# A layer with routed experts: the test for left-over blocks moves behind the output, and the output's tiles change their order

## The chip, the cores and the metric

One core of a Trainium2 chip runs the whole kernel. The metric is the time of one execution on the device, in microseconds; the median of several runs counts. TensorE (PE) multiplies matrices and transposes, VectorE (DVE), ScalarE (ACT) and GpSimd (POOL) compute on tiles of 128 partitions, SyncE (SP) issues most of the DMA transfers. Each of them works through its own list of instructions in order, and they wait for one another by semaphores.

## The reference

One layer over 1024 latent tokens of width 1024 and 256 context tokens: a token mixer (an mLSTM part and a convolution part), then a mixture of 64 experts of which every token takes 8, with one shared expert. Float32 throughout. What the change touches is the end:

```python
def body(acc, xs):
    rows, rw, e = xs
    xb = hpad[rows]
    y = (jax.nn.silu(xb @ we_gate[e]) * (xb @ we_up[e])) @ we_down[e]
    return acc.at[rows].add(y * rw[:, None].astype(y.dtype)), None
...
shared = (jax.nn.silu(hf @ ws_gate) * (hf @ ws_up)) @ ws_down
return (acc[:nt] + shared).reshape(B, T, D)
...
x = x + mx[5] * _rms_norm(_moe_ffn(hx, ...), g_post_ffn[l])
```

## The kernel before, in words

`Full.run` calls `front` and `mixer_out` (the mixer and the routing), then `moe`, `spill` and `final`. The change lies in the last three.

**The schedule.** How many rows each expert gets is known only on the chip. The program is built with fixed capacities: a table of blocks (`BLOCKS`) of up to 128 rows, each with its expert's rank by load. The routing gives the blocks their experts and rows. What does not fit into the table is left over; `route` counts the blocks of 128 rows that it makes up into `nl`.

**The blocks.** `pipeline` runs over the table: gather rows of `hx` from DRAM, transpose them (`stage_x`: transposes on TensorE into `px`, a rounded copy `xH` by ScalarE, the remainder `xL` by VectorE), multiply with gate and up weights (`stage_gu`: 24 matmuls of 512 columns into `pgu`, SiLU into `sgu`, product `hgu`), transpose the result (`stage_ht`: `pht`, then `hTH` and `hTL`), multiply with the down weights (`stage_dn`: 12 matmuls into `py`), and add the rows to one of two arrays in DRAM, `acc0` or `acc1`, by an accumulating scatter from POOL. A product of full precision is three matmuls of rounded parts (`mm3`, lines 436 to 438). The shared expert of token tiles 0 to 3 (`SE = 4`) is in the table, that of tile 3 as its last block, whose result is added to rows 384 to 511 of `acc1` by a plain accumulating DMA (line 1557). That of tiles 4 to 7 is left to the end. `pipeline` closes with loads for the end: the rows `h` of tiles 4 to 7 and `x1`, the residual, of all eight; and it transposes tiles 4 and 5.

**The left-over blocks.** `spill` reads `nl` from memory into a register on every engine and branches over its body where `nl` is 0. The body makes up the lists of rows again and loops over the blocks, one expert's weights each, adding to `acc0`. In this data nothing is left over, and the body is not run.

```python
nl = nc.values_load(self.nl[0:1, 0:1], min_val=0, max_val=128)
with tc.If(nl > 0):
```

**The output.** `final` goes over the eight tiles in their order. For each, `sums` loads its 128 rows of `acc0` and `acc1` (`v0`, `v1`; three buffers each, `VB = 3`). Tiles 4 to 7 get their shared expert: `gu` one tile ahead, then `stage_ht` and 12 matmuls, and VectorE adds the two halves `py` to `v0` (line 1727). Then VectorE adds `v1` (line 1729), and `rms_apply` makes the output: squares summed on ScalarE (line 1143), the product with the weight `vg` on POOL (line 1145; for the last tile on VectorE), the power -1/2 of the mean on POOL (line 1147, `ssf`), and `u`, the scaled product plus `x1`, on VectorE (line 1148). SP stores it (line 1732). The squares and `vg` have one buffer each:

```python
junk, t = [fp.tile([128, D], F32, name=m, bufs=1) for m in ("sq", "vg")]
```

**What orders the work.** Within a stretch of straight code a scheduler puts each engine's instructions into an order of its own, by what depends on what and its estimate of their times. It does not move them over a branch. Every engine follows that order, and waits where its next instruction has to.

Of the kernel before, what the change touches and what calls it, by code (L numbers as in the profile page):

```python
# [869 lines left out]
SE = 4  # L870
# [9 lines left out]
NA = 2  # L880
VB=3
# [4 lines left out]
class Full(Layer):  # L886
    known = SH

    def run(self):
        nc, tc, A = self.nc, self.tc, self.A  # L890
        cp, cp_ = self.pool("const", 1)
        dp, dp_ = self.pool("dram", 1, DRAM)
        self.hx = dp.tile([NX, XW], F32, name="hxd")
        self.x1d = dp.tile([NX, D], F32, name="x1d")
        self.posd = dp.tile([128, 8, NE], F32, name="posd")
        self.acc = [dp.tile([NX, D], F32, name=f"acc{k}") for k in range(NA)]
        self.rowd = dp.tile([2, NR, 128], F32, name="rowd")
        self.amd = dp.tile([4, D], F32, name="amd")
        ct, ct_ = self.pool("ctmp", 1)
        self.consts(cp, ct)  # L900
        self.route_consts(cp, ct)
        self.close(ct_)
        X = self.front(cp)
        self.mixer_out(cp, X)
        self.moe(cp)
        self.spill()
        self.final(cp)
        self.close(self.fin_)
        self.close(dp_)
        self.close(cp_)  # L910
# [49 lines left out]
    def mixer_out(self, cp, X):  # L960
# [45 lines left out]
        pI = pp.tile([128, HM * NE], F32, name="pI")  # L1006
        run = cp.tile([128, NE], F32, name="run")
        nc.vector.memset(run, 0.0)
        self.run = run
        r8 = lambda v: v.rearrange("p (k t) -> p k t", k=8)  # L1010
# [61 lines left out]
        def place(j, pl, mask, eq):  # L1072


            mm(pl[:, 1], self.sub, mask, start=True, stop=True)
            mm(pl[:, 2], self.onb, mask, start=True, stop=True)
            nc.vector.tensor_tensor(self.pos[:, j], pl[:, 1], run, op=OP.add)
            nc.vector.tensor_tensor(run, run, pl[:, 2], op=OP.add)
            m = tp.tile([128, TK, NE], F32, name="m")
            (nc.vector if j == 7 else nc.gpsimd).tensor_tensor(  # L1080
                m, eq, self.pos[:, j].unsqueeze(1).to_broadcast([128, TK, NE]), op=OP.mult)
            p8 = tp.tile([128, 3, TK], F32, name="p8")
            nc.vector.tensor_reduce(p8[:, 0], m, axis=AX.X, op=OP.add)
            pi = tp.tile([128, 2, TK], I32, name="pi")
            nc.vector.tensor_copy(pi[:, 0], p8[:, 0])
            nc.vector.tensor_scalar(pi[:, 1], pi[:, 0], -HB, None, op0=OP.bitwise_and)
            nc.vector.tensor_tensor(p8[:, 1], p8[:, 0], pi[:, 1], op=OP.subtract)
            nc.vector.tensor_tensor(p8[:, 2], self.f8[:, j], pi[:, 1], op=OP.add)
            oh = tp.tile([128, TK, HB], BF, name="oh")
            nc.vector.tensor_tensor(oh, self.io[:, :HB].unsqueeze(1).to_broadcast([128, TK, HB]), e8(p8[:, 1]),  # L1090
                                    op=OP.is_equal)
            l1 = tp.tile([128, TK, 128], BF, name="l1")
            nc.scalar.activation(l1[:, :, :HB], oh, AF.Identity, scale=self.pc)
            nc.gpsimd.tensor_scalar(l1[:, :, HB:], oh, float(j), None, op0=OP.mult)
            g = tp.tile([128, TK, HM * NE], BF, name="g", bufs=1)
            for k in range(TK):
                n = HM * NE if j + k == 0 else min(2 * (j + 1), HM) * NE
                nc.vector.tensor_scalar(g[:, k, :n], self.ioh[:, :n], p8[:, 2, k:k + 1], None, op0=OP.is_equal)
            return l1, g
# [147 lines left out]
    def spill(self):  # L1247

        nc, tc, A = self.nc, self.tc, self.A
        mm = nc.tensor.matmul  # L1250
        nl = nc.values_load(self.nl[0:1, 0:1], min_val=0, max_val=128)
        with tc.If(nl > 0):
# [47 lines left out]
            x = T("oxg", [128, XW])  # L1300
            nc.vector.memset(x, 0.0)
            with tc.For_i(0, nl, 1) as i:
# [20 lines left out]
                h = T("oh", [128, DE])  # L1323
# [16 lines left out]
                                             bounds_check=NX - 1, oob_is_err=False, compute_op=OP.add)  # L1340
            self.close(tp_)
            self.close(op_)

    def row_weight(self, junk, x, e, out):

        n = out.shape[0]
        self.nc.vector.scalar_tensor_tensor(junk[:n], self.io[:n, :NE], e[:n], x[:n, D:], op0=OP.is_equal, op1=OP.mult,  # L1347
                                            accum_out=out)
# [215 lines left out]
    def pipeline(self, experts):  # L1564

        nc, mp = self.nc, self.mp
        n, total = len(BLOCKS), 3 * len(experts)
# [64 lines left out]
        def row(key):  # L1632

            if not self.halves:
                t = take(F32, "rows", 0, NF)
                self.halves = [t[:, :D], t[:, D:]]
            self.rows[key] = self.halves.pop()
            return self.rows[key]
# [49 lines left out]
        split(total, True)  # L1688
        for j in range(SE, 8):
            nc.sync.dma_start(row(("h", j)), self.hx[128 * j:128 * j + 128, :D])  # L1690
        self.x = {j: self.stage_x(self.rows["h", j]) for j in range(SE, min(SE + 2, 8))}
        for j in range(8):
            nc.sync.dma_start(row(("x", j)), self.x1d[128 * j:128 * j + 128])
        self.shared = [W[3 * shared + c] for c in range(3)]


    def final(self, cp):
        nc, tc, A = self.nc, self.tc, self.A
        fp, fp_ = self.pool("last", 2)

        def sums(j):
            out = []
            for k in range(NA if j < 8 else 0):
                out.append(fp.tile([128, D], F32, name=f"v{k}", bufs=VB))
                nc.sync.dma_start(out[k], self.acc[k][128 * j:128 * j + 128])  # L1705
            return out

        def gu(j):
            if j + 2 < 8:
                self.x[j + 2] = self.stage_x(self.rows["h", j + 2])  # L1710
            return self.stage_gu(self.x[j], self.shared)

        V = [sums(n) for n in range(VB - 1)]
        if SE < 8:
            h = gu(SE)
        for j in range(8):
            V.append(sums(j + VB - 1))
            v, x1 = V[j], self.rows["x", j]
            if j >= SE:
                hT = self.stage_ht(h)  # L1720
                if j < 7:
                    h = gu(j + 1)
                for q in range(2):
                    py, s = self.bank("py", 512), slice(512 * q, 512 * q + 512)
                    for k in range(2):
                        self.mm6(py, hT, self.shared[2], k, 2, slice(k * 1024 + q * 512, k * 1024 + q * 512 + 512))
                    nc.vector.tensor_tensor(v[0][:, s], v[0][:, s], py, op=OP.add)  # L1727
            for u in v[1:]:
                nc.vector.tensor_tensor(v[0], v[0], u, op=OP.add)  # L1729
            junk, t = [fp.tile([128, D], F32, name=m, bufs=1) for m in ("sq", "vg")]  # L1730
            self.rms_apply(fp, v[0], self.fin, x1, junk, t, x1, "f", nc.gpsimd if j < 7 else None)
            nc.sync.dma_start(self.out[128 * j:128 * j + 128], x1)
        self.close(fp_)
        for _, p in self.pps[::-1]:
            self.close(p)
        for _, p in self.units[NF - 1:1:-1]:
            self.close(p)
        self.close(self.mp_)
        for _, p in self.units[1::-1]:
            self.close(p)  # L1740
        self.close(self.gp_)
# [69 lines left out]
```

## Time and profile before

| | |
|---|---|
| median of 3 runs | 1500.9 us (1499.1 to 1502.76) |
| profiled execution | 1497.91 us |
| its span, first to last instruction | 1496.1 us |
| mean granted TensorE clock | 0.986 |
| busy: PE, DVE, ACT, POOL | 1426.1, 1133.3, 753.7, 477.9 us |

The profile is of one execution. An engine's busy time says little about a short stretch: over the whole run TensorE is busy 95% of the span, but the change concerns some 65 us at its end, from the last expert block to the last store. There the order of time of each engine and the chain of waits tell more. Times in rows count from the span's start. "PEldq", "DVEq" and so on are the sequencers of the engines, which read registers, branch and wait for semaphores; "SPq" is the queue of SP, where DMA transfers are issued.

### The profile page before, as it was taken

To read this page: it belongs to the slowest core of one execution; us is meant where nothing else is said; L and a number is where in the kernel's file an instruction comes from. 1 tells how busy PE (TensorE), PEld (TensorE's weight loads), DVE (VectorE), ACT (ScalarE), POOL (GpSimd) and SP (SyncE) were. 2 spreads that over 40 slices of the span, in tenths; PEclk is the share of its full clock that TensorE was granted. 3 is DMA by queue.
4 is the path that set the end of the run, shared out by engine and by line. 5 is a ranking of instruction groups with operands and counts; after the bars stand their busy time and mean duration, and the time that the engine had idled before them with its cause. 6 is when DMAs were issued, how large, how long until landed. Compare 5 with 4: busy or idle time off the path is not lost. (4 is left out here: it accounts for less than half of the span.)

```text
span 1496.1 us, 22962 instructions
## 1 busy us (share of the span) xinstructions
PE 1426.1 (95%) x8211; PEld 1088.5 (73%) x8211; DVE 1133.3 (76%) x1942; ACT 753.7 (50%) x1241; POOL 477.9 (32%) x306
## 2 busy tenths in 40 slices
PE   6999999989999989999999999999999999999975
PEld 4688997765567755876788888888777777777764
DVE  5899979767867886744678788888777877777636
ACT  4421011245433344644566666776676767666621
POOL 1245001112213422233333333333334344455324
PEclk9999999999999999999999999999999999999998
DMA  8421051018653567997999999999999999999975
GB/s 314 176 71 43 1 189 40 19 48 287 221 187 115 193 240 275 357 294 246 306 288 327 331 322 319 333 343 339 316 342 299 321 342 310 315 352 318 337 251 209
DMA packets 94385, 371.64 MB, mean 248 GB/s; under 512 B 18269, under 2 KB 26789, under 8 KB 67770
## 3 DMA queue, kind: packets, MB, share of 16 engines
q1 hardware_dynamic: 65946, 298.48, 53.3%
q0 software_dynamic: 26032, 70.19, 19.2%
q10 hardware_dynamic: 2288, 1.45, 0.4%
q8 instruction: 66, 1.08, 0.3%
q14 instruction: 53, 0.43, 0.1%
HBM read 322.38 MB, written 62.19 MB: 257 GB/s over the span
## 5 line engine op out<-in xcount | busy, mean ns | idle before, releaser
L51 DVE TENSOR_TENSOR u<-u,u 128x1024 fp32r<-128x1024 f32 x354 | 422.0, 1220 | 124.7 <-ACT u L50 94.8
L50 ACT CAST u<-u 128x1024 fp32r<-128x1024 f32 x354 | 361.3, 1052 | 108.5 <-PE pgu L438 41.6
L1559 POOL DMA_INDIRECT acc<-yb,dst x98 | 194.4, 1983 | 351.7 <-ACT hTH L50 118.3
L436 PE MATMUL pgu<-u,xH 128*128 128x512 f32 x608 | 245.8, 404 | 0.4
L437 PE MATMUL pgu<-u,xH 128*128 128x512 f32 x608 | 238.8, 393 | 0.0
L438 PE MATMUL pgu<-u,xL 128*128 128x512 f32 x608 | 238.1, 392 | 0.0
L1439 POOL DMA_INDIRECT xg<-hxd,tok x98 | 123.6, 1261 | 194.1 <-DVE rwj L1347 68.6
L431 DVE SCALAR_TENSOR_TENSOR X<-X,cw 128x912 f32<-128x912 f32 (+14 forms) x120 | 152.0, 1291 | 1.1
L436 PEld LDWEIGHTS pgu<-u,xH 128*128 128x128 f32 x608 | 114.5, 188 | 25.5 <-ACT u L50 2.6
L438 PEld LDWEIGHTS pgu<-u,xL 128*128 128x128 f32 x608 | 114.3, 188 | 24.6
L437 PEld LDWEIGHTS pgu<-u,xH 128*128 128x128 f32 x608 | 114.5, 188 | 21.5
L436 PE MATMUL py<-u,hTH 128*128 128x512 f32 x304 | 122.1, 402 | 0.5 <-ACT hTH L50 0.5
L437 PE MATMUL py<-u,hTH 128*128 128x512 f32 x304 | 119.8, 394 | 0.0
L438 PE MATMUL py<-u,hTL 128*128 128x512 f32 x304 | 118.6, 395 | 0.0
L436 PE MATMUL pf<-hH,wfH 128*128 128x512 f32 x256 | 103.6, 408 | 0.0
L437 PE MATMUL pf<-hL,wfH 128*128 128x512 f32 x256 | 102.7, 401 | 0.7 <-DVE hL L226 0.6
L51 DVE TENSOR_TENSOR xL<-px,xH 128x512 fp32r<-128x512 f32 x152 | 97.5, 681 | 7.7 <-ACT xH L50 7.3
L438 PE MATMUL pf<-hH,wfL 128*128 128x512 f32 x256 | 102.3, 400 | 0.0
L50 ACT CAST xH<-px 128x512 fp32r<-128x512 f32 x152 | 83.9, 592 | 13.7 <-PE pgu L437 7.8
L1551 DVE COPY yb<-py 128x512 f32<-128x512 f32 x75 | 51.5, 687 | 46.3 <-PE py L438 45.8
L51 POOL TENSOR_TENSOR wfL<-wfr,wfH 128x1024 fp32r<-128x1024 f32 x14 | 48.0, 3428 | 118.2 <-ACT wfH L50 104.2
L1461 PE MATMUL px<-ident,xg 128*128 128x128 f32 x600 | 83.8, 274 | 1.1 <-DVE nl L1244 1.1
(431 smaller groups left out, 2515.6 us busy)
## 6 DMA issues: line engine op xcount, KB each, us to landing
u<-in_we_dram SPq DMA_DIRECT2D x192, 1024.0 KB
wa<-in_wa_dram SPq DMA_DIRECT2D x64, 256.0 KB
wa<-in_wa_dram SPq DMA_DIRECT2D x8, 1024.0 KB
wfr<-in_wf_dram SPq DMA_DIRECT2D x16, 512.0 KB
v<-acc SPq DMA_DIRECT2D x16, 512.0 KB
acc<-zero SPq DMA_DIRECT2D x13, 512.0 KB
u<-in_ws_dram SPq DMA_DIRECT2D x6, 1024.0 KB
X<-in_xT_dram SPq DMA_DIRECT2D x8, 512.0 KB
```

Of the source, the lines that this page charges most:

```text
L50: self.nc.scalar.copy(H, src)
L51: return (eng or self.nc.vector).tensor_tensor(L, src, H.bitcast(F32), op=OP.subtract).ins
L431: nc.vector.scalar_tensor_tensor(y[:, :, a:b], u[:, :, a + o:b + o], cw[:, i:i + 1], y[:, :, a:b], op0=OP.mult, op1=OP.add)
L436: mm(out, lH, rH, start=start, stop=False, skip_group_check=free)
L437: mm(out, lH, rL, start=False, stop=False, skip_group_check=free)
L438: mm(out, lL, rH, start=False, stop=stop, skip_group_check=free)
L1439: nc.gpsimd.indirect_dma_start(out=x[:n], out_offset=None, in_=self.hx, in_offset=bass.IndirectOffsetOnAxis(ap=self.tok[:n, c:c + 1], axis=0),
L1461: nc.tensor.transpose(pt[:, k], x[:, (4 * q + k) * 128:(4 * q + k) * 128 + 128], self.ident)
L1551: nc.vector.tensor_copy(y[:, 512:], py)
L1559: nc.gpsimd.indirect_dma_start(out=self.acc[b % NA].rearrange("r (n d) -> (r n) d", n=n), in_=y[:rows], in_offset=None, out_offset=bass.In ...
```

## The change

`spill` is called behind the output. The output's loop moves from `final` into a function of its own, `tiles`, which `final` calls first; the body of `spill` then loads `x1` again and calls `tiles` a second time, so that with blocks left over the whole output is made again. The first transposes of tiles 4 and 5 move from `pipeline` into `tiles`. And the tiles come in the order 4, 0, 5, 1, 6, 2, 7, 3: `order` puts one of the tiles that need the shared expert ahead of each that doesn't. POOL's product is now made for all but the last in that order, which is tile 3.

```diff
--- before.py
+++ after.py
@@ -903,7 +903,6 @@
         X = self.front(cp)
         self.mixer_out(cp, X)
         self.moe(cp)
-        self.spill()
         self.final(cp)
         self.close(self.fin_)
         self.close(dp_)
@@ -1340,6 +1339,9 @@
                                              bounds_check=NX - 1, oob_is_err=False, compute_op=OP.add)
             self.close(tp_)
             self.close(op_)
+            for j in range(8):
+                nc.sync.dma_start(self.rows["x", j], self.x1d[128 * j:128 * j + 128])
+            self.tiles()
 
     def row_weight(self, junk, x, e, out):
 
@@ -1688,34 +1690,38 @@
         split(total, True)
         for j in range(SE, 8):
             nc.sync.dma_start(row(("h", j)), self.hx[128 * j:128 * j + 128, :D])
-        self.x = {j: self.stage_x(self.rows["h", j]) for j in range(SE, min(SE + 2, 8))}
         for j in range(8):
             nc.sync.dma_start(row(("x", j)), self.x1d[128 * j:128 * j + 128])
         self.shared = [W[3 * shared + c] for c in range(3)]
 
 
-    def final(self, cp):
-        nc, tc, A = self.nc, self.tc, self.A
+    def tiles(self):
+
+
+        nc = self.nc
         fp, fp_ = self.pool("last", 2)
+        order = [j for k in range(8 - SE) for j in (SE + k, *range(k * SE // (8 - SE), (k + 1) * SE // (8 - SE)))]
+        later = [j for j in order if j >= SE]
+        x = {j: self.stage_x(self.rows["h", j]) for j in later[:2]}
 
         def sums(j):
             out = []
-            for k in range(NA if j < 8 else 0):
+            for k in range(NA):
                 out.append(fp.tile([128, D], F32, name=f"v{k}", bufs=VB))
                 nc.sync.dma_start(out[k], self.acc[k][128 * j:128 * j + 128])
             return out
 
         def gu(j):
             if j + 2 < 8:
-                self.x[j + 2] = self.stage_x(self.rows["h", j + 2])
-            return self.stage_gu(self.x[j], self.shared)
-
-        V = [sums(n) for n in range(VB - 1)]
-        if SE < 8:
-            h = gu(SE)
-        for j in range(8):
-            V.append(sums(j + VB - 1))
-            v, x1 = V[j], self.rows["x", j]
+                x[j + 2] = self.stage_x(self.rows["h", j + 2])
+            return self.stage_gu(x.pop(j), self.shared)
+
+        h = gu(SE)
+        V = [sums(j) for j in order[:VB - 1]]
+        for n, j in enumerate(order):
+            if n + VB - 1 < 8:
+                V.append(sums(order[n + VB - 1]))
+            v, x1 = V[n], self.rows["x", j]
             if j >= SE:
                 hT = self.stage_ht(h)
                 if j < 7:
@@ -1728,9 +1734,13 @@
             for u in v[1:]:
                 nc.vector.tensor_tensor(v[0], v[0], u, op=OP.add)
             junk, t = [fp.tile([128, D], F32, name=m, bufs=1) for m in ("sq", "vg")]
-            self.rms_apply(fp, v[0], self.fin, x1, junk, t, x1, "f", nc.gpsimd if j < 7 else None)
+            self.rms_apply(fp, v[0], self.fin, x1, junk, t, x1, "f", nc.gpsimd if n < 7 else None)
             nc.sync.dma_start(self.out[128 * j:128 * j + 128], x1)
         self.close(fp_)
+
+    def final(self, cp):
+        self.tiles()
+        self.spill()
         for _, p in self.pps[::-1]:
             self.close(p)
         for _, p in self.units[NF - 1:1:-1]:
```

What this makes of the engines' lists is seen at three places. Buffers carry numbers: before, `v0_15113`, `15117`, `15166`, `15208` and `15222` are tiles 0, 1, 2, 5 and 6; in the changed kernel `v0_14529`, `14533`, `14537` and `14619` are tiles 4, 0, 5 and 1.

SP, from the test on, before (ahead of it stand the loads of `x1`, and between them and this piece the body that is skipped):

```order
L1252 UNCONDITIONAL_BRANCH
L1705 DMA v0_15113<-acc0_63 128x1024
L1705 DMA v1_15115<-acc1_64 128x1024
L1705 DMA v0_15117<-acc0_63 128x1024
L1705 DMA v1_15119<-acc1_64 128x1024
L1705 DMA v0_15166<-acc0_63 128x1024
L1705 DMA v1_15168<-acc1_64 128x1024
L1732 DMA out_0_dram<-u6_14465 128x1024
```

The same place in the changed kernel, from the last loads of `x1` on:

```order
L1694 DMA u8_14439<-x1d_61 128x1024 x2
L1694 DMA u11_14442<-x1d_61 128x1024 x2
L1711 DMA v1_14531<-acc1_64 128x1024
L1711 DMA v1_14535<-acc1_64 128x1024
L1711 DMA v1_14539<-acc1_64 128x1024
L1711 DMA v0_14529<-acc0_63 128x1024
L1711 DMA v0_14533<-acc0_63 128x1024
L1711 DMA v0_14537<-acc0_63 128x1024
L1711 DMA v1_14621<-acc1_64 128x1024
L1711 DMA v1_14635<-acc1_64 128x1024
L1711 DMA v0_14619<-acc0_63 128x1024
```

The branch is gone from between the loads of `x1` and those of the sums, `acc1` comes first for three tiles, then `acc0`, and tile 4 is the first of each three.

VectorE, its first instructions behind the test, before (`px_15123` and `px_15130` are the transposed halves of tile 6, `pgu_15137` belongs to tile 4):

```order
L1729 TENSOR_TENSOR v0_15113<-v0_15113,v1_15115 128x1024
L1146 TENSOR_SCALAR ssf_15173<-ssf_15173 128x1
L1148 SCALAR_TENSOR_TENSOR u6_14465<-vg_15172,ssf_15173,u6_14465 128x1024
L51 TENSOR_TENSOR xL_15122<-px_15123,xH_15121 128x512
L51 TENSOR_TENSOR xL_15122<-px_15130,xH_15121 128x512
L1498 TENSOR_TENSOR hgu_15164<-pgu_15137,sgu_15162 128x256
L1729 TENSOR_TENSOR v0_15117<-v0_15117,v1_15119 128x1024
L1729 TENSOR_TENSOR v0_15166<-v0_15166,v1_15168 128x1024
```

In the changed kernel, behind the second half of tile 5's split (`px_14486` and `px_14493` are tile 6, `px_14550` and `px_14557` tile 7; `pgu_14500` and `pgu_14564` belong to tiles 4 and 5):

```order
L51 TENSOR_TENSOR xL_14469<-px_14477,xH_14468 128x512
L1735 TENSOR_TENSOR v0_14533<-v0_14533,v1_14535 128x1024
L51 TENSOR_TENSOR xL_14485<-px_14486,xH_14484 128x512
L51 TENSOR_TENSOR xL_14485<-px_14493,xH_14484 128x512
L1500 TENSOR_TENSOR hgu_14527<-pgu_14500,sgu_14525 128x256
L51 TENSOR_TENSOR hTL_14545<-pht_14541,hTH_14544 128x256
L51 TENSOR_TENSOR xL_14549<-px_14550,xH_14548 128x512
L51 TENSOR_TENSOR xL_14549<-px_14557,xH_14548 128x512
L1500 TENSOR_TENSOR hgu_14591<-pgu_14564,sgu_14589 128x256
L1733 TENSOR_TENSOR v0_14529<-v0_14529,py_14593 128x512
```

One sum, that of tile 0, still stands ahead of tile 6's split; the sums of the next two tiles and the first output have gone from behind it, and the work of tiles 4 and 5 takes their place.

VectorE in the middle of the output, before, from tile 5's output to tile 6's sum:

```order
L1148 SCALAR_TENSOR_TENSOR u8_14471<-vg_15362,ssf_15363,u8_14471 128x1024
L1498 TENSOR_TENSOR hgu_15404<-pgu_15377,sgu_15402 128x256
L1727 TENSOR_TENSOR v0_15222<-v0_15222,py_15406 128x512
L1727 TENSOR_TENSOR v0_15222<-v0_15222,py_15414 128x512
L51 TENSOR_TENSOR hTL_15436<-pht_15432,hTH_15435 128x256
L1729 TENSOR_TENSOR v0_15222<-v0_15222,v1_15224 128x1024
```

In the changed kernel, from tile 4's output to tile 5's sum (`py_14673` and `py_14681` are tile 5's halves, `pgu_14644` belongs to tile 6):

```order
L1147 SCALAR_TENSOR_TENSOR u8_14439<-vg_14611,ssf_14612,u8_14439 128x1024
L1145 TENSOR_SCALAR ssf_14626<-ssf_14626 128x1
L1147 SCALAR_TENSOR_TENSOR u6_14433<-vg_14625,ssf_14626,u6_14433 128x1024
L1500 TENSOR_TENSOR hgu_14671<-pgu_14644,sgu_14669 128x256
L1733 TENSOR_TENSOR v0_14537<-v0_14537,py_14673 128x512
L1735 TENSOR_TENSOR v0_14619<-v0_14619,v1_14621 128x1024
L1733 TENSOR_TENSOR v0_14537<-v0_14537,py_14681 128x512
L51 TENSOR_TENSOR hTL_14721<-pht_14717,hTH_14720 128x256
L1735 TENSOR_TENSOR v0_14537<-v0_14537,v1_14539 128x1024
```

Two outputs now follow each other, those of tiles 4 and 0, and behind the second stand the product of tile 6, both halves and the sum of tile 5, and the sum of tile 1.

## Rows read from the trace of the kernel before

**Rows 1.** TensorE in order of time: start, us, engine, line, operation, tiles, [idle before]

```profile
1431.30 0.82 PE L1461 MATMUL px<-ident,u 128*128 128x128 f32 x6
...
1439.93 1.94 PE L1461 MATMUL px<-ident,u 128*128 128x128 f32 x8 [6.20 <-DVEq L1252]
...
1465.60 0.39 PE L436 MATMUL pgu<-u,xH 128*128 128x512 f32 x1
1465.84 0.39 PE L437 MATMUL pgu<-u,xH 128*128 128x512 f32 x1
```

**Rows 2.** Sequencers at lines 1251 and 1252: ns min/median/max, first and last start

```profile
L1251 DVEq TENSOR_LOAD <-nl x1: 1719/1719/1719, 1434.4 to 1434.4; - x1
...
L1252 PEldq COMPARE_BRANCH  x1: 5473/5473/5473, 1433.7 to 1433.7; - x1
...
L1252 DVEq EVENT_SEMAPHORE  x1: 21/21/21, 1439.7 to 1439.7; - x1
```

**Rows 3.** Waits of the DMA queue of SP, 1405 to 1445: us, times, longest

```profile
SPq L1705 <- DVEq L1252: 4.7, 1, 4.7
```

**Rows 4.** Chain of waits, in order of time: start us, us, what

```profile
1442.70 8.26 DMA v<-acc
...
1464.85 2.41 POOL vg L1145
1467.25 0.52 POOL ssf L1147
...
1467.83 1.17 issue
```

**Rows 5.** VectorE in order of time: first sum, one tile, last two outputs

```profile
1445.80 1.22 DVE L1729 TENSOR_TENSOR v<-v,v 128x1024 f32<-128x1024 f32 x1 [10.72 <-DMA v<-acc]
...
1478.83 1.28 DVE L1148 SCALAR_TENSOR_TENSOR u<-vg,ssf,u 128x1024 f32<-128x1024 f32 x1 [1.65 <-POOL ssf L1147]
1480.03 0.42 DVE L1498 TENSOR_TENSOR hgu<-pgu,sgu 128x256 f32<-128x256 f32 x1
1480.36 1.27 DVE L1727 TENSOR_TENSOR v<-v,py 128x512 f32<-128x512 f32 x2
1481.56 0.42 DVE L51 TENSOR_TENSOR hTL<-pht,hTH 128x256 fp32r<-128x256 f32 x1
1481.89 1.22 DVE L1729 TENSOR_TENSOR v<-v,v 128x1024 f32<-128x1024 f32 x1
...
1487.16 1.28 DVE L1148 SCALAR_TENSOR_TENSOR u<-vg,ssf,u 128x1024 f32<-128x1024 f32 x1 [0.44 <-POOL ssf L1147]
...
1490.14 1.28 DVE L1148 SCALAR_TENSOR_TENSOR u<-vg,ssf,u 128x1024 f32<-128x1024 f32 x1 [0.44 <-POOL ssf L1147]
```

**Rows 6.** POOL in order of time: the last scatters and the last accumulate

```profile
1420.38 1.56 POOL L1559 DMA_INDIRECT acc<-yb,dst  x1 [3.20 <-ACT yb L1540]
1428.37 1.56 POOL L1559 DMA_INDIRECT acc<-yb,dst  x1 [6.42 <-ACT hTH L50]
1432.71 0.96 POOL L1557 DMA_DIRECT2D acc<-yb  x1 [2.79 <-ACT xH L50]
```

**Rows 7.** DMA queues, 1433:1434, 1434:1437, 1446:1449: packets, MB, share of engines

```profile
q1 hardware_dynamic: 2, 0.00, 1.1%
...
q0 software_dynamic: 118, 0.46, 99.4%
...
q1 hardware_dynamic: 346, 1.25, 101.9%
```

**Rows 8.** Groups by line, 1435 to 1496: the cast (busy us, mean ns)

```profile
L50 ACT CAST xH<-px 128x512 fp32r<-128x512 f32 x4 | 2.1, 579 | 0.0
```

**Rows 9.** Windows: length, busy PE PEld DVE ACT POOL, granted clock, DMA share, GB/s

```profile
1440.00:1442.50 2.50, 2.50 (x10) 2.33 (x11) 0.00 (x0) 0.00 (x0) 0.00 (x0) 0.50 0.60 213
```

**Rows 10.** The queue of SP in order of time, from 1490

```profile
1491.45 0.33 SPq L1732 DMA_DIRECT2D out_dram<-u  x1
```

**Rows 11.** Records of line 1807, the closing: durations ns, first and last start

```profile
L1807 POOLq DRAIN  x3: 46/112/6605, 1488.6 to 1495.8; - x3
```

## Prediction, made before the changed kernel was run

> **What bounds the kernel now.** The change touches only what comes after the last expert block, so I read that stretch: first TensorE's own order of time, then the sequencers at the branch, then the chain of waits, then VectorE, then the DMA work under it.
>
> TensorE, still busy at 1431.30, stands idle for the 6.20 us before 1439.93, so from 1433.7 [rows 1]. The sequencers say why [rows 2]. Reading the count `nl` and branching over the body that is never run takes TensorE's sequencer 5.47 us in the branch alone; VectorE's begins to read `nl` at 1434.4, needs 1.72, and the next thing it does is at 1439.7. The loads of the sums stand behind that: SP's queue waited 4.7 us for VectorE's sequencer [rows 3]. Turned round, 1439.7 - 4.7 = 1435.0 is when all else that they wait for, the last scatter into `acc0` among it, was there. So the test holds TensorE back by 6.2 us and the loads by 4.7.
>
> From there a chain through POOL and VectorE ends last, and hardly touches TensorE. One tile of output in the chain of waits reads [rows 4]: 2.41 (`vg`, the product with the weight, on POOL), 0.52 (`ssf`, the power, POOL), 1.17 of `u` (the output, VectorE); then VectorE adds the next tile's two sums (`v`, 1.22 [rows 5]), 5.5 with the handoffs. `vg` has one buffer, so the next `vg` waits for `u`. The first sum starts at 1445.80 and the last `u` starts at 1490.14 and ends at 1491.42 [rows 5]: **45.6 us from first sum to last output**. The store and the closing barrier take the other 4.7 of the span.
>
> **The change, part by part.** Nothing ahead of the last expert block moves; every engine has there the instructions that it had. Work for a positive `nl` is made and skipped as before.
>
> *The loads start sooner, but not by 4.7.* SP now goes on from the x1 loads straight to three loads of `acc1`. Their last scatter (by the order of POOL's list) was issued at 1420.38, eight microseconds ahead of the one into `acc0` (1428.37) that was there by 1435.0 [rows 6], so they are issued before 1433, when the load queue runs empty (two packets left in that microsecond [rows 7]). From 1433 on the engines then have this to do: three `acc1` loads, 1.57 MB at the 1.25 MB per 3 us of full engines, 3.8 us; the last accumulate, issued at 1432.71, which alone filled 99.4% of 3 us, 3.2 with its edges; and of the `acc0` loads the ones of tiles 4 and 0, 1.05 MB, 2.5 us [rows 6, 7]. That is 9.5 us, to 1442.5, and 0.7 for the landing: tile 0's sum starts at 1443.2 (now 1445.80). Bounds: if the accumulate yields entirely it is 3.8 + 2.5 + 0.7, so 1440.0. At the other end I take all of the extra that six loads show now: 3.15 MB are 7.5 us of work, but landed at 1450.96 (1442.70 + 8.26), 11.1 after the first issue [rows 4], 3.6 in place of my 0.7: 1446.1. I take 1443.2, since the queue is full already and the 3.6 is mostly the way to a first packet.
>
> Of the accumulate the Trainium skill ("DMA: Bandwidth & Descriptors", Queues, rings and completion order) says that a DMA engine goes round-robin between the queues that have work. By that rule the loads share with it, as summed here; served first they would give 1440.0. No row of this run has both queues full at that place.
>
> *TensorE starts sooner, and is stopped again.* VectorE works in order, and its list now puts the addition for tile 0, which waits for the loads, ahead of the two halves of tile 6's split `xL`. TensorE needs the first of these before it may transpose tile 7, six matmuls into tile 5's. At 0.23 us a matmul (starts 1465.60 and 1465.84 [rows 1]) and 0.82 for six transposes, its thirty matmuls (7.0) and twelve transposes (1.6) after 1433 bring it there by about 1442, so the 6.2 us won turn into a wait for tile 0's sum. From that sum: addition 1.1, `xL` 0.6 and a handoff 0.1; transposes of tiles 7 and 4's `h` 1.3; the remaining 18 matmuls 4.1; then 1.0 for one cast of tile 7 (0.58 [rows 8]) and two handoffs; and VectorE's row for tiles 7, 5 and 4 at the intervals of [rows 5]: two `xL` 1.2, `hgu` 0.33, two `py` 1.2, `hTL` 0.33, the sum 1.2, handoff 0.14. Together **12.6 us from the first sum to POOL's first `vg`**, which is now of tile 4 (POOL's list has it first). Now it is the length of one addition, since tile 0 needs nothing from TensorE.
>
> *The tiles.* From [rows 4, 5]: `vg` to `u` is 2.95; `u` passes in 1.20. A tile whose sum is already made follows its predecessor by 2.95 + 1.28 and a handoff, 4.35. Tile 0 after tile 4 is one. But `hgu` of tile 6, tile 5's two `py`, tile 1's sum, `hTL` and tile 5's sum all stand behind tile 0's `u` on VectorE; in the kernel before, `hgu` and `py` of the next tile stand ahead of the `u`, under POOL's time. So tile 5 follows by 2.95 + 1.20 + 0.33 + 0.60 + 1.13 + 0.60 + 0.33 + 1.22 + 0.14 = 8.5. A pair costs 12.9, and not twice 5.5. The second pair likewise without `hgu` and `hTL`: 12.2. Tiles 2 and 7 have their sums ahead: 8.7. From tile 7's `vg` to the end of tile 3: 2.95 and the 4.26 from the start of the last `u` but one to the end of the last (1487.16 to 1491.42 [rows 5]), 7.2. Sum **41.0**.
>
> *The clock.* After its 6.2 us idle TensorE had a granted clock of 0.50 (of the two levels, 1.2 GHz) from 1440 to 1442.5 [rows 9]. Such a gap now lies late, ahead of tile 7's last twelve matmuls: +0.7, between 0 and 1.5.
>
> So the last `u` ends at 1443.2 + 12.6 + 41.0 + 0.7 = 1497.5, against 1491.42.
>
> *The test at the end.* On TensorE, ScalarE and POOL it lies under the last tiles. On VectorE it cannot start before the last `u`: then 1.0 to have `nl` (of the 1.72, which began while a split was still running), and 3.6 as now from 1436.1 to 1439.7 [rows 2]: `u` + 4.6. Now the end waits for the last store, issued at 1491.45 [rows 10], and the rest after `u` is 4.7 in all, of which the store is some 3.1. So the end is 1.5 later. Bounds: 0, if the way over the body takes no longer than the store; and +5.3, if POOL's closing drain, 6.6 us long and begun with its last power [rows 11], is that long by itself and starts only after the test (then some 10 us follow `u`, and not 4.7).
>
> For the price of such a test the Trainium skill ("Advanced Engine Details and Errata", Control Flow Timing) gives about 108 ns for a compare-and-branch. By that the end would cost nothing. The rows say 5.47 us on one sequencer and 3.6 on another for the same branch, and here they decide; "Runtime: NRT & Kernel Launch" (Instruction fetch mechanics) has the reason that fits them, a taken branch whose target must be fetched by DMA first.
>
> **Sum.** Span 1497.5 + 4.7 + 1.5 = 1503.7, against 1496.1: **+7.6 us**. The profiled execution took 1497.91 beside a median of 1500.9 (it is at the low end of the runs), so it would be 1505.5; on the median, 1508.5. About 0.2% (3 us) is what a measurement of this kernel can tell from no change.
>
> **Rivals.**
> 1. *Faster.* Loads and TensorE start up to 4.7 and 6.2 us sooner, and the tiles keep their pace. With the sum at 1440.5 and 45.6 from there, as now, the last `u` is at 1486.1 and the span 1492.3: -3.8, 1497.1. It decides on the first `vg`: to gain, it must start before 1491.4 - 41.0 - 1.5 = 1448.9; I have 1455.8, and 1453.1 with the earliest loads. For it speaks that the branch really is the last wait there. Against it, POOL's list begins with tile 4, which needs all of TensorE's work on two tiles. 5%.
> 2. *No change to be told.* Loads early (TensorE then bounds the first sum at 1440.5), no loss by the clock, and the last branch under the store: 1440.5 + 12.6 + 41.0 + 4.7 = 1498.8, +2.7: 1503.6. 12%.
> 3. *Worse by the end.* The forecast, but POOL's drain follows the test: +5.3 in place of 1.5, span 1507.5, +11.4: 1512.3. 15%.
> 4. *The change doesn't do what it says.* Were `nl` positive, the tiles would run twice, some 50 us more. The trace of before has no instruction of the body, so no.
>
> **How the numbers follow.** The forecast has 68%, and 1508.5. The low end is rival 2 less a little, 1502; the high end takes latest loads (+2.9), clock (+0.8) and half of the drain's extra, 1514. Left out are rival 1, part of 2 and what lies above: under 2 in 10. Slower by over 0.2%: forecast and rival 3, 83%; within: 12%; faster: 5%.
>
> **What would show it.** Right: TensorE works on from 1433 without the 6 us gap, then waits near 1442 for `xL`; the first `vg` at 1453-1458; starts of `vg` in pairs, 4.4 and 8 us apart; VectorE's last `u` at 1495-1500; over 5.5 us from there to the end. Wrong: a first `vg` before 1449, or tiles 5.5 us apart throughout; then the gain at the test stays, and the kernel is faster.

## The result, and the profile after

| | before | changed |
|---|---|---|
| median of the runs, us | 1500.9 (7 runs, 1495.37 to 1502.76) | 1506.54 (7 runs, 1504.53 to 1513.88) |
| ratio of the runs | 1 | 1.0067, 95% interval 1.0048 to 1.0086 |
| profiled execution, its span | 1497.91, 1496.1 | 1509.4, 1507.6 |
| POOL's last accumulate is issued | 1432.71 | 1432.19 |
| VectorE's first sum, after that | 13.1 | 11.8 |
| POOL's first `vg`, after that | 14.4 | 26.6 |
| end of VectorE's last `u`, after that | 58.7 | 69.1 |
| end of the span, after that | 63.4 | 75.4 |

The changed kernel is slower: the ratio says 10 us (7 to 13). The two medians lie only 5.6 us apart, and in the two profiled executions the tail is 12.0 us longer (63.4 and 75.4); the profiled execution of the changed kernel is one of its longer ones. One of the twelve executions of e12 below took 2586.07 us at a granted clock of 0.811, and its ratio leaves that one out. What comes ahead of the tail shifts by some us from one execution to the next, so here and below I count from the moment POOL issues the last accumulate into `acc1` (in [rows 6] at 1432.71).

TensorE in order of time, on both sides of the new stop (start, duration, idle before it and what ended that):

```profile
1439.43 0.39 PE L438 MATMUL pgu<-u,xL 128*128 128x512 f32 x1
1445.82 1.12 PE L1463 MATMUL px<-ident,u 128*128 128x128 f32 x4 [6.01 <-DVE xL L51]
...
1449.30 0.63 PE L436 MATMUL pgu<-u,xH 128*128 128x512 f32 x1
1449.72 0.63 PE L437 MATMUL pgu<-u,xH 128*128 128x512 f32 x1
...
1450.84 0.40 PE L437 MATMUL pgu<-u,xH 128*128 128x512 f32 x1
1451.07 0.40 PE L438 MATMUL pgu<-u,xL 128*128 128x512 f32 x1
```

The 6.20 us for VectorE's sequencer [rows 1] are gone, and 6.01 us for `xL` have come where that gap used to end. Behind the stop matmuls start 0.42 us apart instead of 0.23, until 1450.6. The windows around it say what clock was granted (columns as in [rows 9]):

```profile
1440.00:1446.00 6.00, 0.18 (x1) 0.18 (x2) 2.06 (x3) 0.00 (x0) 0.00 (x0) 0.81 0.50 202
1446.00:1451.00 5.00, 5.00 (x18) 4.29 (x19) 1.12 (x3) 0.37 (x1) 0.00 (x0) 0.54 0.36 105
```

VectorE in order of time shows what the stop is behind, and further down what stands between two tiles:

```profile
1443.94 1.23 DVE L1735 TENSOR_TENSOR v<-v,v 128x1024 f32<-128x1024 f32 x1 [9.39 <-DMA v<-acc]
1445.08 1.28 DVE L51 TENSOR_TENSOR xL<-px,xH 128x512 fp32r<-128x512 f32 x2
...
1466.01 1.28 DVE L1147 SCALAR_TENSOR_TENSOR u<-vg,ssf,u 128x1024 f32<-128x1024 f32 x1 [2.94 <-POOL ssf L1146]
1467.21 0.42 DVE L1500 TENSOR_TENSOR hgu<-pgu,sgu 128x256 f32<-128x256 f32 x1
1467.55 0.68 DVE L1733 TENSOR_TENSOR v<-v,py 128x512 f32<-128x512 f32 x1
1468.14 1.22 DVE L1735 TENSOR_TENSOR v<-v,v 128x1024 f32<-128x1024 f32 x1
1469.28 0.68 DVE L1733 TENSOR_TENSOR v<-v,py 128x512 f32<-128x512 f32 x1
1469.88 0.42 DVE L51 TENSOR_TENSOR hTL<-pht,hTH 128x256 fp32r<-128x256 f32 x1
1470.21 1.22 DVE L1735 TENSOR_TENSOR v<-v,v 128x1024 f32<-128x1024 f32 x1
...
1488.64 2.81 DVE L1735 TENSOR_TENSOR v<-v,v 128x1024 f32<-128x1024 f32 x1
```

The sum of tile 0 waited 9.39 us for its loads with `xL` of tile 6 behind it; and after tile 0's `u`, 4.2 us of work follow before POOL has its next input (tile 5's halves and sum, and between them steps of tiles 6 and 1). POOL's products (four of seven) and one power:

```profile
1458.74 2.41 POOL L1144 TENSOR_TENSOR vg<-v,fin 128x1024 f32<-128x1024 f32 x1 [25.59 <-DVE v L1735]
...
1463.09 2.38 POOL L1144 TENSOR_TENSOR vg<-v,fin 128x1024 f32<-128x1024 f32 x1 [1.40 <-DVE ssf L1145]
...
1471.57 2.41 POOL L1144 TENSOR_TENSOR vg<-v,fin 128x1024 f32<-128x1024 f32 x1 [5.59 <-DVE v L1735]
...
1490.33 1.53 POOL L1146 TENSOR_TENSOR ssf<-ssf,mhalf 128x1 f32<-128x1 f32 x1
...
1493.26 3.26 POOL L1144 TENSOR_TENSOR vg<-v,fin 128x1024 f32<-128x1024 f32 x1 [1.40 <-DVE u L1147]
```

The third of these, tile 5's, waited for its sum (`DVE v`): the buffer of `vg` was free again when tile 0's `u` had ended, 4.3 us earlier.

The chain of waits ahead of the first sum (start, length), where [rows 4] had one DMA wait of 8.26:

```profile
1427.84 7.95 DMA acc<-yb,dst
...
1436.28 7.58 DMA v<-acc
```

And POOL's sequencer at the test and at the kernel's closing line (ns shortest/median/longest, first and last start), the latter to be set beside [rows 11]:

```profile
L1251 POOLq INC_SWDGE_SEM  x1: 1418/1418/1418, 1500.2 to 1500.2; - x1
...
L1817 POOLq DRAIN  x3: 46/107/5095, 1501.7 to 1507.3; - x3
```

### The profile page after: what moved, and what is told of

It reads as the page before. It is cut to its first block, busy times and chain, and to the rows that moved or that the text cites. A ratio compares the mean times of both kernels' runs of the same rounds, so it can differ in the third digit from the quotient of the medians.

```text
span 1507.6 us, 22951 instructions
## 1 busy us (share of the span) xinstructions
PE 1427.4 (95%) x8205; PEld 1088.9 (72%) x8211; DVE 1134.9 (75%) x1942; ACT 754.3 (50%) x1241; POOL 476.1 (32%) x306
## 4 chain that ended last, share of the span: by engine, by line
PE 77%; DVE 8%; DMA 6%; issue 4%; POOL 3%; ACT 2%; SPq 0%; POOLq 0%; ACTq 0%; DVEq 0%
PE pgu L436 9%; PE pgu L437 9%; PE pgu L438 9%; PE pgu L1488 5%; PE py L436 4%; PE py L438 4%; PE py L437 4%; PE px L1463 4%; PE pf L436 4%; PE pf L437 3%; PE pf L438 3%; PE py L1540 2%; DMA wa<-in_wa_dram 2%; DMA xg<-hxd,tok 2%; PE pa L756 2%
```

## The experiments

My theory after the result: (T1) the order of the tiles makes the loss, not the test's new place; within the order (T2) TensorE's second stop and (T3) the work that stands behind each early tile's `u` on VectorE are two separate losses; (T4) the test at the end costs the 1.5 us more between last `u` and end. The rivals stand in what was expected of each run. All twelve, in us after POOL's last accumulate, from one profiled execution each; the ratio compares 6 to 12 runs of each with runs of the kernel before:

| | first sum | first `vg` | last `u` ends | span ends | ratio, 95% interval |
|---|---|---|---|---|---|
| before | 13.1 | 14.4 | 58.7 | 63.4 | 1 |
| changed | 11.8 | 26.6 | 69.1 | 75.4 | 1.0067 (1.0048 to 1.0086) |
| e1 order alone | 17.4 | 27.3 | 69.9 | 74.6 | 1.0068 (1.0041 to 1.0095) |
| e2 test alone | 10.0 | 11.5 | 58.3 | 64.5 | 1.0000 (0.9979 to 1.0020) |
| e3 no test | 11.4 | 25.5 | 68.0 | 72.7 | 1.0056 (1.0034 to 1.0078) |
| e4 split first | 11.0 | 18.2 | 60.7 | 67.0 | 1.0027 (1.0009 to 1.0045) |
| e5 pairs ahead | 11.6 | 26.2 | 65.4 | 71.7 | 1.0044 (1.0022 to 1.0067) |
| e6 two `vg` | 10.8 | 25.2 | 68.2 | 73.8 | 1.0074 (1.0047 to 1.0102) |
| e9 = e4 + e5 | 11.6 | 18.2 | 57.5 | 63.7 | 1.0002 (0.9984 to 1.0019) |
| e7 natural, split first, `u` later | 9.9 | 11.4 | 54.4 | 60.7 | 0.9994 (0.9971 to 1.0017) |
| e8 = e7 + two `vg` | 9.7 | 11.1 | 57.1 | 64.1 | 0.9997 (0.9973 to 1.0021) |
| e10 feed | 10.0 | 11.5 | 57.4 | 64.1 | 1.0015 (0.9998 to 1.0032) |
| e11 = e10 + `u` later | 9.9 | 11.4 | 56.8 | 63.0 | 1.0011 (0.9993 to 1.0029) |
| e12 = e10 + `vg` on VectorE | 10.1 | 11.5 | 51.5 | 58.3 | 0.9972 (0.9951 to 0.9994) |

**e1: the order alone.** The kernel before with the changed kernel's list `order`:

```diff
-        for j in range(8):
-            V.append(sums(j + VB - 1))
-            v, x1 = V[j], self.rows["x", j]
+        for n, j in enumerate(order):
+            if n + VB - 1 < 8:
+                V.append(sums(order[n + VB - 1]))
+            v, x1 = V[n], self.rows["x", j]
```

> The kernel before with the tiles' order alone changed to 4 0 5 1 6 2 7 3; the test stays where it was, ahead of the output, and the transposes of tiles 4 and 5 stay ahead of it. Theory (the pairs cost, through VectorE's order): TensorE starts at about 1440 as before, with some 2.5 us at the lower clock, and needs 18.5 us of work of its own and its neighbours to the first vg of tile 4, so 1459.7; from there 41 to 43 us to the end of the last u (pairs 12.9 and 12.2 apart) and 4.7 to the end: span near 1505.5 to 1507, median about 1510 (+9). No second stop of TensorE, since here its list puts tile 6's split ahead of tile 0's sum. Rival A (the order costs nothing by itself; what made the changed kernel slower is the test at its end and the second stop): about 1501, within 2 of the kernel before.

Measured 1.0068, and the first `vg` at 27.3: the theory. TensorE in order of time has the old stop here, and not the new one:

```profile
1433.95 1.94 PE L1461 MATMUL px<-ident,u 128*128 128x128 f32 x8 [6.38 <-DVEq L1252]
```

So the order costs the whole 10 us with the test at either end. With the first `vg` at 27.3 and 26.6, less than 1 us is left of the 6 us that TensorE gained by the test's move; the rest went into its new stop.

**e2: the test alone.** The changed kernel with the old order:

```diff
-        order = [j for k in range(8 - SE) for j in (SE + k, *range(k * SE // (8 - SE), (k + 1) * SE // (8 - SE)))]
+        order = list(range(8))
```

> The changed kernel with the tiles in the order 0 to 7 again; the test stays last. Theory: the loads' early start gives first sum at about 1443.9 (1.9 earlier than before); 45.6 us from there to the last u's end as before, so 1489.5; the end costs 6.2 in place of 4.7. Span 1495.7 to 1497.5, median about 1501 (0 to +1 against before, 5 below the changed kernel). Rival A (the end and the second stop cost it, the order nothing): TensorE is stopped here too, even longer, by sums ahead of tile 6's split, so as slow as the changed kernel, about 1506. Rival B (the early start passes on in full, and the end costs nothing): 1498.

Measured 1.0000: the theory's end of the range. Rival A falls by the time. Rival B's 3 us less lies within the interval; it falls by the profile. The first `vg` comes 2.9 earlier than before, but tiles 4 to 6 come 7.4 to 8.3 apart, as each one's `py`, and the `hgu` of the tile after it, stand behind its predecessor's `u` (T3 again), and the end is 1.6 longer: nothing is left. TensorE has its new stop here too, and a longer one:

```profile
1447.51 1.11 PE L1463 MATMUL px<-ident,u 128*128 128x128 f32 x4 [8.88 <-DVE xL L51]
```

The time is that of the kernel before all the same, which had its 6.20 us for the test instead. The first four tiles need nothing from TensorE here, so the stop doesn't hold up the first `vg`.

**e3: no test.** Blocks behind the schedule are left out.

```diff
         self.tiles()
-        self.spill()
```

> The changed kernel without the test and what it guards (blocks behind the schedule are not handled at all). Theory: POOL's closing drain is then bound to its last power, as before, and ends some 5.1 us after it, so the end comes 4.7 to 5.5 after the last u and not 6.2: 1 to 1.7 us less than the changed kernel, about 1505. Rival A (the end is the main cost): 4 to 5 us less, 1501 to 1502. Rival C (the test at the end costs nothing, as its work lies under the store and the drain): no difference, 1506.5.

Measured 1.0056, 1.6 us under the changed kernel by the ratios (their intervals overlap); from last `u` to the end 4.7 against 6.3, as in the kernel before. Rival A's 4 to 5 us less lies at the edge of the interval; against it and against rival C stands the profile. POOL's drain here:

```profile
L1816 POOLq DRAIN  x3: 46/107/6599, 1498.0 to 1505.2; - x3
```

It begins with the last power (1498.07, 1.46 long) and ends at 1504.6, 5.1 after that power; in the kernel before the same 5.1 (6605 ns from 1488.65, power done at 1490.11). In the changed kernel it is 5095 ns from 1501.7, behind the test's last instruction on POOL. In all three the drain ends 5.1 us after whatever POOL did last, and the test moved that by some 1.6; 1.42 of it is the `INC_SWDGE_SEM` shown above, behind the branch.

**e4: tile 6's split ahead of the sums.** `x6` is the last instruction of that split, and `issue_after` puts what follows behind it in the generated list:

```diff
-            for u in v[1:]:
-                nc.vector.tensor_tensor(v[0], v[0], u, op=OP.add)
+            with self.tc.issue_after(self.x6):
+                for u in v[1:]:
+                    nc.vector.tensor_tensor(v[0], v[0], u, op=OP.add)
```

> The changed kernel, only VectorE's list changed: every addition of a tile's two sums comes after tile 6's split (tile 0's was ahead of it). Theory: TensorE no longer stops near 1440 for xL and has no low clock after it; the first vg comes at about 1451.5 in place of 1458.7, and the tiles keep their pairs (12.9 and 12.2 apart, 41 to 43 us in all): 6 to 7 us less than the changed kernel, about 1500. Rival D (the tiles' pace is set by the loads or by TensorE further on, so an earlier first vg is given back): first vg earlier, but no more than 2 us less at the end, 1504.5 to 1506.5.

Measured 1.0027, 6 us under the changed kernel: the theory. The window at the place of the stop, full of work and at the full clock:

```profile
1444.00:1450.00 6.00, 6.00 (x28) 4.85 (x27) 3.77 (x6) 1.36 (x3) 0.00 (x0) 1.00 0.42 144
```

The first `vg` comes 8.4 earlier: the stop's 6.0, and 2.4 that go with the low clock after it (5.0 us at 0.54, as shown above, are 2.3 us lost against the full clock). From the first `vg` to the last `u` it is 42.6 as in the changed kernel.

**e5: `u` behind the next sum.** For tiles 0, 1 and 2 the last step is kept in `held` and emitted after the sum of the next tile:

```diff
+            for fin, i, y in held:
+                with self.tc.issue_after(last):
+                    fin()
+                nc.sync.dma_start(self.out[128 * i:128 * i + 128], y)
+            held.clear()
```

> The changed kernel, only the place of three outputs in VectorE's list changed: u of tiles 0, 1 and 2 comes right behind the sum of the next tile that needs TensorE (5, 6, 7), and no longer ahead of that tile's hgu, py, hTL and sum. The second stop of TensorE stays. Theory (a pair costs 12.9 because that work stands behind u): it now lies under POOL's vg and power, the starts of vg come 4.4 to 5 apart throughout, the pairs 9 to 10, and the last u ends 6 to 9 sooner: about 1499 to 1501. Rival E (vg has one buffer, or TensorE has not finished by then, and that sets the pair): pairs stay at 12 to 13, 0 to 2 less than the changed kernel.

Measured 1.0044, 3.5 us less (the intervals overlap; in the profile the last `u` ends 3.7 sooner): the theory's direction at half its size. The `vg` of tiles 4, 5 and 6, and from VectorE tile 1's sum and tile 0's `u`:

```profile
1458.05 2.41 POOL L1144 TENSOR_TENSOR vg<-v,fin 128x1024 f32<-128x1024 f32 x1 [25.21 <-DVE v L1736]
...
1469.23 2.43 POOL L1144 TENSOR_TENSOR vg<-v,fin 128x1024 f32<-128x1024 f32 x1 [2.93 <-DVE u L1147]
...
1478.82 3.26 POOL L1144 TENSOR_TENSOR vg<-v,fin 128x1024 f32<-128x1024 f32 x1 [1.40 <-DVE u L1147]
```

```profile
1463.87 2.01 DVE L1736 TENSOR_TENSOR v<-v,v 128x1024 f32<-128x1024 f32 x1 [0.45 <-DMA v<-acc]
...
1467.87 1.28 DVE L1147 SCALAR_TENSOR_TENSOR u<-vg,ssf,u 128x1024 f32<-128x1024 f32 x1
```

Pairs of 11.2 and 9.6, not 12.8 and 12.1, but 10.4 for the third (it was 9.6). VectorE was busy for nearly all of the 8.1 us from tile 4's `u` (1461.04) to the end of tile 0's, tile 1's sum being one of the steps (2.01, after 0.45 for a load). I had costed the list as if it lay under POOL's time; it is as long as that.

**e6: two buffers for `vg`.**

```diff
-            junk, t = [fp.tile([128, D], F32, name=m, bufs=1) for m in ("sq", "vg")]
+            junk, t = [fp.tile([128, D], F32, name=m, bufs=n) for m, n in (("sq", 1), ("vg", 2))]
```

> The changed kernel with two buffers for vg in place of one, so that the next product need not wait for u. The generated list of VectorE stays as it was, tile 0's u ahead of tile 5's hgu, py and sum; POOL's list has both products of a pair ahead of its two powers. Theory: the pair is 12.25 (7.9 to tile 0's u, 4.35 from there to the next product), so only 1 to 2 less than the changed kernel. Rival E (the one buffer sets the pair): pairs of 8.5 to 9, 7 to 8 less, about 1499.

Measured 1.0074, nothing gained: pairs of 12.9 and 12.6. Rival E falls. My 1 to 2 us less lie within the interval, but the pairs didn't shorten: both products of a pair now run ahead of both powers, so tile 0's `u` starts 7.4 after tile 4's product (1460.10 and 1467.46) where it was 7.3, and the rest of the pair stands behind that `u` as before.

**e9: e4 and e5 together.**

> The two edits together that each took something off the changed kernel: the sums behind tile 6's split (6 us by the ratios), and the three outputs behind the next sums (3.5). Theory (two separate losses, one before the first vg, one in the row of pairs): they add up, 9 to 10 less than the changed kernel, ratio to the kernel before 1.000 to 1.002. Rival G (both act on the same wait, TensorE's end): no more than the larger of the two, ratio 1.0025 to 1.004.

Measured 1.0002. 9.7 us less than the changed kernel, 6.0 and 3.5 apart: T2 and T3 are separate losses and add up; rival G falls.

**e7 and e8: what would beat both.** Natural order, e4's edit, and each tile's `u` held behind the next tile's sum; e8 with e6's edit too. Against e9, e7 has the order 0 to 7 and:

```diff
-            wait = j < SE and n < 7
+            wait = n < 7
```

> A version that would beat both: the test last, tiles 0 to 7 in order, all sums behind tile 6's split on VectorE, and each tile's u right behind the sum of the tile after it. Theory: the early start is kept (first vg 11 to 12 us after POOL's last accumulate, 14.4 in the kernel before), tiles 5.3 apart for the first three and 4.4 to 5 after that, the last tile bound by TensorE, which is done some 45 us after that accumulate; the last u ends at about 50 in place of 58.7, the end costs 6.2 in place of 4.7: 5 to 9 faster than the kernel before. Rival F (vg takes 3.3 and not 2.4 beside VectorE's additions, and TensorE's waits and lower clock give the rest back): within 3 of the kernel before.

> The one before with two buffers for vg as well. Theory: the first four tiles come 4 to 4.5 apart in place of 5.3, but the last tile still waits for TensorE, so 0 to 2 less than that one. Rival E (the one buffer for vg bounds the row of tiles): 5 or more less than that one.

Neither can be told from the kernel before: rival F, and e8 gained nothing on e7. VectorE of e7 shows why:

```profile
1444.24 5.69 DVE L1739 TENSOR_TENSOR v<-v,v 128x1024 f32<-128x1024 f32 x3 [1.59 <-DMA v<-acc]
...
1449.92 0.41 DVE L51 TENSOR_TENSOR hTL<-pht,hTH 128x256 fp32r<-128x256 f32 x1
...
1460.21 1.28 DVE L1147 SCALAR_TENSOR_TENSOR u<-vg,ssf,u 128x1024 f32<-128x1024 f32 x1 [2.75 <-POOL ssf L1146]
1461.41 0.42 DVE L1500 TENSOR_TENSOR hgu<-pgu,sgu 128x256 f32<-128x256 f32 x1
```

Three sums take 5.69 ahead of `hTL`, and `hgu` stands behind a `u` that waits for POOL. TensorE stopped at both (2.66 and 3.90 us), each time with the lower clock soon after (0.50 from 1452.5 to 1455.0, 0.51 from 1461.8 to 1464.0).

**e10 and e11: TensorE's inputs first.** Tile 5's `hgu` and tile 4's `hTL` ahead of the loop, the sums and the first `u` behind them (the core of the edit); e11 adds e7's `held` from tile 3 on.

```diff
+        h, hT = {SE: gu(SE)}, {}
+        hT[SE] = self.stage_ht(h.pop(SE))
+        h[SE + 1] = gu(SE + 1)
...
+            with self.tc.issue_after([first, second, third][min(n, 2)]):
+                for u in v[1:]:
+                    last = nc.vector.tensor_tensor(v[0], v[0], u, op=OP.add).ins
```

> Test last, tiles 0 to 7 in order, and the output written so that TensorE's inputs stand first on VectorE: tile 5's gate and up product and tile 4's hTL are made ahead of the loop, the sum of tile 0 stands behind tile 6's split, that of tile 1 behind hTL, that of tile 2 and the first u behind tile 7's split and tile 5's hgu; each later tile's hTL and hgu are made one tile ahead. Theory (e7 and e8 gained nothing because three sums stood ahead of hTL, and a u ahead of hgu: TensorE stopped twice, 6.6 to 9.7 us, with the lower clock after each): without these stops TensorE is done 41 to 44 us after POOL's last accumulate (46 to 48 in e7), tiles come 5.3 apart, the last u ends 51 to 53 after it (58.7 in the kernel before), 4 to 6 faster than the kernel before, ratio 0.996 to 0.9975. Rival H (the row of tiles on VectorE and POOL is the bound, whatever TensorE does): ratio 0.9985 to 1.001.

> The one before, and from tile 3 on each u right behind the sum of the tile after it. Theory: as TensorE is no longer waited for, the last four tiles come 4.4 to 5 apart and not 5.3 to 7.4: 1 to 3 less than that one. Rival H: no difference.

By the time, rival H for both. But the theory wasn't put to the test: the edit was to take TensorE's stops away, and TensorE still stopped (3.0, 3.0 and 1.1 us in e10), with its last matmul 46.6 after the accumulate, where 41 to 44 was expected. That the row of tiles bounds the time whatever TensorE does isn't shown. One reason is seen where POOL and VectorE of e10 start together:

```profile
1443.01 2.40 POOL L1144 TENSOR_TENSOR vg<-v,fin 128x1024 f32<-128x1024 f32 x1 [10.53 <-DVE v L1744]
```

```profile
1443.03 3.45 DVE L1744 TENSOR_TENSOR v<-v,v 128x1024 f32<-128x1024 f32 x1
```

A sum of 1.22 takes 3.45 when it starts just after a `vg`: 2.38 until that product ends, and about its own time after it. So a product on POOL takes VectorE's time too, where the two meet; where the sum starts first, the product is the longer one (3.28 at 1451.12).

**e12: the product on VectorE.** e10 with one edit:

```diff
-            fin = self.rms_apply(fp, v[0], self.fin, x1, junk, t, x1, "f", nc.gpsimd if n < 7 else None, wait)
+            fin = self.rms_apply(fp, v[0], self.fin, x1, junk, t, x1, "f", None, wait)
```

> e10 with one edit: the product vg of every tile on VectorE, none on POOL (before, the last tile's alone). Theory (in e10 a sum that began with a vg took 3.45 us and not 1.22, and a vg beside a sum 3.3 and not 2.4: the two engines shut each other out, so VectorE's 1.22 for sum and 1.28 for u and POOL's 2.4 for vg follow one another, 4.9 a tile and 5.4 with the power, whatever the order): with vg at 1.22 on VectorE a tile's three passes take 3.7, eight tiles 30, the other work for four tiles 12; the last u ends 48 to 51 us after POOL's last accumulate (57.3 in e10, 58.7 in the kernel before), and the ratio to the kernel before is 0.993 to 0.997. Rival J (the two overlap well enough, and 8.6 us more work on the engine that is waited for lengthens its row): the last u ends as late as in e10 or later, ratio 1.000 to 1.004.

Measured 0.9972 (0.9951 to 0.9994): faster than the kernel before, and 6 us under e10; the last `u` ends at 51.5; both lie just outside what I gave. VectorE where e10 had the 3.45:

```profile
1442.47 1.21 DVE L1144 TENSOR_TENSOR vg<-v,fin 128x1024 f32<-128x1024 f32 x1
...
1443.67 1.21 DVE L1744 TENSOR_TENSOR v<-v,v 128x1024 f32<-128x1024 f32 x1
```

7 x 1.22 us more work on the engine that is waited for, and the row of tiles is 6 us shorter: rival J falls. The first of TensorE's stops shrinks with it, in e10 and then here:

```profile
1449.91 0.44 PE L1518 MATMUL pht<-ident,hgu 128*128 128x128 f32 x2 [3.00 <-DVE hgu L1500]
```

```profile
1448.31 0.44 PE L1518 MATMUL pht<-ident,hgu 128*128 128x128 f32 x2 [1.27 <-DVE hgu L1500]
```

What share of the 6 us each part has stays open. The edit ends the waiting of the two engines for each other, but it also cuts each product from 2.4 to 1.22 and lets POOL make the power without a product ahead of it. Nor was the kernel before run with this edit alone.

## Why the prediction was right, point by point

The forecast (slower, +7.6, 1508.5) holds: the median is 1506.54, and the ratio says 10 us. Direction and mechanism are borne out by the runs. That the median came within 2 us is in part luck: in the profiled executions the tail grew by 12.0, and the four terms of the sum all fell short, by 1.3, 2.2, 0.9 and 0.1. By its steps:

- *The loads start sooner, but not by 4.7.* Right in sign, mis-sized: first sum 11.8 after the accumulate, forecast 10.5. I let three loads of `acc1` start by 1433; SP issued the first at 1428.20, 0.4 after the scatter into `acc0`, on which the other loads wait. That scatter was there 3.6 after the accumulate's issue (1427.84 + 7.95), and by 2.3 in the kernel before. That the loads slowed it is argued, not shown. It doesn't explain the miss: in e2 the scatter is there just as late (3.7), and with tile 0 first in the order the sum comes at about 10 all the same (e2, e7, e10).
- *TensorE starts sooner, and is stopped again.* Right: same place and same cause; e1 and e4 show it from both sides. The stop is 6.01 us long where the forecast's numbers give 3.0 (from 1442 to 1445.0), for TensorE ran dry at 1439.8. And VectorE's list didn't have to change for it: in the kernel before, too, tile 0's sum and its `u` stood ahead of tile 6's split, but TensorE came there later and waited only 1.02 us (until 1452.03).
- *The clock.* The step that failed in size. I had a low clock only late, +0.7, although [rows 9] show it after just such a gap; this stop brought one too. From first sum to first `vg` it took 14.8, forecast 12.6. Nearly all of the difference lies in TensorE's stretch behind the stop, the transposes and 18 matmuls: 7.5 (1445.82 to 1453.3), forecast 5.4. e4 prices stop and clock together at 8.4.
- *The tiles.* Pairs of 12.83 and 12.14, forecast 12.9 and 12.2. The third step took 9.55 (8.7) and the rest 8.07 (7.2). For the third, a sum that met a `vg` took 2.81 and held POOL's next power to 1.53 (0.55 elsewhere); for the rest, the last `vg` met a sum and took 3.26. In all 42.6, forecast 41.0 and 0.7. The cause given (the next tile's work behind `u`) is confirmed by e5; against the single buffer stand e6 and the wait of tile 5's `vg` shown above; what moving that work would give back I had too high, as VectorE is nearly full there.
- *The test at the end.* 6.3 from last `u` to the end, forecast 6.2; the number was right and the reason wrong, so this term is luck. VectorE was over the body at 1503.6, 2.3 after its last `u` (forecast 4.6). Neither that nor the store decides, but POOL's closing drain, 5.1 us after POOL's last instruction (e3), which ended at 1506.8. Rival 3 named the drain, but priced it as if its 6.6 us were all to come after the test.
- *Rivals.* Rival 1 asked for a first `vg` before 1448.9; it came at 1458.74. e2 shows that even with one 11.5 after the accumulate (1444.2 in the kernel before) the time stays the same. Of the signs given for being right, the first `vg` (1453 to 1458) and the last `u` (1495 to 1500, it started at 1500.04) were missed by less than 1 us.

## What to carry to other kernels

When a wait is removed at the head of an engine's queue, read the lists of its neighbours next: TensorE's 6 us went into the next thing that stood in VectorE's way, with a stretch at the lower clock behind the stop as before. What such a stop holds up depends on the order: with tile 4 first, 6.0 us put the first `vg` off by 8.4; with tile 0 first, the first `vg` came 2.9 early in spite of 8.9 us (e2). An engine in order passes a late operand on to all that is listed behind it, so what feeds TensorE belongs ahead of additions that wait for DMA. And before work is handed to POOL to relieve VectorE, see what VectorE's instructions take while POOL runs: here taking it back was worth 6 us (e12 against e10).

## What was not expected of the hardware

- VectorE's addition of two SBUF tiles and POOL's product wait for each other: 1.22 becomes 3.45 (e10), 2.4 becomes 3.26 (the changed kernel). The Trainium skill ("SBUF — State Buffer", Who interferes with whom) has the rule: a VectorE instruction with two SBUF inputs contends with a GpSimd instruction that reads SBUF, the ports that they share are an exclusive lock, and the order of issue decides who is blocked. The trace agrees: the one that starts second takes longer by about what the first has left. By that rule the last two terms of the forecast's row of tiles (8.7 and 7.2) would have been longer. The additions of `py`, with one input in PSUM, kept their 0.68 in e10 beside a `vg` (1461.25 and 1461.02).
- POOL's drain at the kernel's end: it ends 5.1 us after POOL's last instruction in the kernel before, the changed one and e3, and the span ends 0.8 to 0.9 after it.
- A stop of TensorE of 6.0 us put the first `vg` off by 8.4 (e4), the 2.4 over its length going with the lower of the two clock levels (1.2 GHz; a granted clock of 0.54 from 1446 to 1451) behind it.
